# A hybrid encoder layer on one core: program order on all four compute engines through the attention, low halves of w_out and q's norms one step later

## The chip, the cores and the metric

The kernel runs on one core of a Trainium2 chip. Its engines work side by side, each through its own queue in order: PE (TensorE, matrix products; its weight loads are shown as PEld), DVE (VectorE), ACT (ScalarE), POOL (GpSimd), and SP, which only issues transfers. The metric is the device time of one execution in microseconds (us); lower is better.

## The reference

One layer over 16 learned meta tokens and two sequences, 256 and 2048 tokens long, with 1024 channels, in float32. Cut to what matters:

```python
h = rmsnorm(z, norm_w)
q, k, v, g_att, c_val, c_glu, g_conv = split(h @ w_in)      # 512,128,128,512,512,512,512
q, k = rmsnorm(q per head, q_norm_w), rmsnorm(k per head, k_norm_w)
att = windowed_gqa(q, k, v, sink) * silu(g_att)   # 8 heads on 2 kv heads, window 128, ALiBi,
                                                  # every query sees the meta keys and a sink logit
cnv = conformer_conv(c_val, c_glu, ...) * silu(g_conv)      # 31-tap depthwise conv, layernorm, silu
y = z + concat(att, cnv) @ w_out                  # meta tokens dropped
```

## The kernel before, in words

Matrix products of float32 data are made of three passes: each operand is split into a high half (a rounded copy, made on ACT) and a low half (the rest, a subtraction on DVE), and hi x hi, hi x lo and lo x hi are added up in psum.

The tokens are 18 blocks of 128, in groups of three. The **projection** (`c_group`, `g_group`, `kv_group`, `q_group`) goes over units of 256 columns of w_in; the convolution's taps on DVE and the layernorms are threaded in between. q, k, v, gates and the convolution's result go to DRAM (`qd`, `kd`, `vd`, `gd`, `cd`). `attention_open` stands ahead of the last unit, the second half of q for the blocks 9 to 17: nine projections (`proj_te`, 24 matmuls of 256 columns each, tile `pj`). After each of these nine, `spread` runs: after the second it transposes q of block 0 (`q_prep`, tile qT), after the third to ninth it does two slots of the attention each and splits one row block of w_out (`split_wo`, lines 289 to 304: two copies on ACT, two subtractions on DVE, two loads for the next but one).

The **attention** goes in rounds (`slot_step`, 8 slots each). Round r computes the scores of block r (tile S, one of 8 pieces a slot, kv 0 in slots 0 to 3 and kv 1 in 4 to 7), and transposes the probabilities of block r-1 in up to 7 banks (tile pT: three for kv 0, one of the meta keys, three for kv 1; blocks at the ends of a sequence have five). It also does two parts of the output projection a slot (tile y, six matmuls) and, in slot 6, transposes q of the next block. At the end of a slot `tick` counts a clock up by one and runs what earlier steps put off with `later(k, ...)`: k ticks later. The pieces, with their engines:

- S is followed after one tick by `bias_max` on DVE (L382: writes sb, and the row minimum nm), after two by `expo` on ACT (L394; with the kv's last piece also L403), after three (last piece) by `norm` (L406, L407 on DVE, then POOL's L408 and four L417).
- A bank pT is followed after one tick by a high copy on ACT (L451, tile ph) and a low half on DVE (L452, tile pl), after two by the pv matmuls (tile O; the meta bank, with L445, L446 and POOL's L462 `pd`, after three).
- A finished O is merged: a copy on ACT (L505, tile tmp), two additions on DVE (L507), a product on POOL (L513), and two ticks later the split L517 and L518 into `rest`, an operand of the output projection. The convolution's part is multiplied on POOL (L526) and split by L533 and L534.
- A finished y is added to z on DVE (L562) and stored. q's transposes are split by two copies on ACT (L347, L348) and two subtractions on DVE (L349, L350).
- q's norm: ACT squares the projection (L897), DVE sums (L898), POOL takes the root (L122, L123), and `fin` (L916, DVE) multiplies one tick later; the result, one of three buffers, is stored two ticks later by SP.

Psum tags have two buffers each: a for S, b for pT and qT, c for O, d for y; in the last unit the nine `pj` take a, b, d, c, d, c, d, c, d.

**What sets the order.** The tile framework orders the instructions of an engine by a list scheduler that plays the program with estimated durations. `manual_schedule` takes engines out of that: they keep the order in which the program issues. `MAN1` (line 50, POOL) holds from `attention_open` to the start of `attention_rest`, `MAN2` (line 51, POOL and PE) from there to the end. SP is always left to the scheduler, except for single instructions held by `keep_in_program_order`. Ahead of `attention_open` all engines are scheduled.

Of the kernel before, what the change touches and what calls it, by code (L numbers as in the profile page):

```python
# [14 lines left out]
ALU = mybir.AluOpType  # L15
# [31 lines left out]
W0 = 3  # L47
LN_WAIT = (9, 2)
LTAGS = "abdcdcdcd"
MAN1 = {mybir.EngineType.Pool}  # L50
MAN2 = {mybir.EngineType.Pool, mybir.EngineType.PE}
QSLOT = 6
MSLOT = 0
QB = 32
# [15 lines left out]
def blk_local(b):  # L70
    g = b // 3
    return g, (NM if g == 0 else 0) + P * (b % 3)
# [3 lines left out]
def hymba_kernel(  # L76
# [13 lines left out]
    nc = tc.nc  # L90
# [45 lines left out]
    def later(k, f):  # L136
        due.setdefault(clock[0] + k, []).append(f)
# [20 lines left out]
    def store(dst, src):  # L158
        later(2, lambda: nc.sync.dma_start(dst, src))
# [12 lines left out]
    phase = [1]  # L172
# [40 lines left out]
    pool, cst, kw, wo, wo_slot, sbs, wraws = {}, {}, [], {}, {}, [], {}  # L213
# [4 lines left out]
    def attention_open():  # L218
# [4 lines left out]
        cst['man'] = man  # L223
        man.enter_context(tc.manual_schedule(engines=MAN1))
        ap = att_pools.enter_context(tc.tile_pool(name="ap", bufs=2, side="right", reuse_waits="tile"))
# [57 lines left out]
    def load_raw(n):  # L283

        for nh in range(2):
            raw = wraws[n, nh] = pool["a"].tile([P, 512], F32, tag="woraw", name=f"woraw{n}_{nh}", bufs=4)
            tc.keep_in_program_order(nc.sync.dma_start(raw, w_out[OUT_ORDER[n]][:, 512 * nh : 512 * nh + 512]))

    def split_wo(n):

        e = OUT_ORDER[n]
        for hl in range(2):
            idx = 2 * n + hl
            if idx % 3 == 0:
                slot = idx // 3
                wo_slot[slot] = xp.tile([P, ND, 400], F32R, tag=("xh", "xl")[slot % 2], name=f"wo{slot}")
            flat = wo_slot[idx // 3].rearrange("p a n -> p (a n)")
            wo[e, hl] = flat[:, D * (idx % 3) : D * (idx % 3) + D]
        for nh in range(2):
            hi, lo = (wo[e, hl][:, 512 * nh : 512 * nh + 512] for hl in range(2))  # L300
            tc.keep_in_program_order(nc.scalar.copy(hi, wraws[n, nh]))
            tc.keep_in_program_order(nc.vector.tensor_tensor(lo, wraws[n, nh], hi, op=ALU.subtract))  # L302
        if n + 2 < 8:
            later(1, lambda: load_raw(n + 2))

    def load_ga(b):
        gat[b] = pool["b"].tile([P, 4, P], F32, tag="ga", name=f"ga{b}", bufs=1)
# [118 lines left out]
    def plan(b):  # L426
        ks = ([0] if has_left(b) else []) + [1] + ([2] if has_right(b) else [])
        return [(k, 0) for k in ks] + [("m", 0)] + [(k, 1) for k in ks]
# [4 lines left out]
    def bank(b, k, kv):  # L433
        pt = psum.tile([P, 4, P], F32, tag="b", name=f"pT{b}_{k}_{kv}")
        if k == "m":
            for i in range(KV):
                nc.tensor.transpose(pt[:, i, :], pmt[b][:, i].rearrange("p a h m -> p (a h m)"), ident)
        else:
            for hl in range(4):
                nc.tensor.transpose(pt[:, hl, :], sbt[b, kv][:, hl, KCOL[k] : KCOL[k] + P], ident)  # L440

        def split():
            if k == "m":
                ph = pool["a"].tile([P, KV, P], F32R, tag="phm", name=f"phm{b}", bufs=1)
                nc.scalar.copy(ph, pt[:, 0:KV, :])  # L445
                nc.vector.tensor_tensor(ph[64:128], pt[64:128, 0:KV, :], ph[64:128], op=ALU.subtract)  # L446
                later(1, lambda: spread_meta(b, ph))
                return
            ph = pool["a"].tile([P, 4, P], F32R, tag="ph", name=f"ph{b}_{k}_{kv}", bufs=3)
            pl = pool["a"].tile([P, 4, P], F32R, tag="pl", name=f"pl{b}_{k}_{kv}", bufs=3)  # L450
            nc.scalar.copy(ph, pt)  # L451
            nc.vector.tensor_tensor(pl, pt, ph, op=ALU.subtract)  # L452
            pv_st[b, k, kv] = (ph, pl)

        later(1, split)
        later(3 if k == "m" else 2, lambda: pv(b, k, kv))

    def spread_meta(b, ph):

        pd = pool["a"].tile([P, KV, 4, P], F32R, tag="pd", name=f"pd{b}", bufs=1)  # L460
        for kv in range(KV):
            nc.gpsimd.tensor_tensor(  # L462
                pd[:, kv],
                ph[:, kv : kv + 1, :].to_broadcast([P, 4, P]),
                cst["msk"].unsqueeze(2).to_broadcast([P, 4, P]),
                op=ALU.mult,
            )
        pv_st[b, "m"] = pd

    def pv_mm(b, kv, lhs, hs, start, stop):  # L470
        if start:
            opj[b, kv] = psum.tile([P, 4, P], F32, tag="c", name=f"O{b}_{kv}")
        o = opj[b, kv]
        for i, t in enumerate(hs):
            nc.tensor.matmul(o, lhs, t, start=(start and i == 0), stop=(stop and i == 1))  # L475

    def pv_meta(b, kv, stop):
        pin(stop)(nc.tensor.matmul)(
            opj[b, kv], cst["vm"][:, kv, :], pv_st[b, "m"][:, kv], start=False, stop=stop
        )  # L480

    def pv(b, k, kv):
        if k == "m":
            pv_meta(b, 0, True)
            later(1, lambda: merge(b, 0))
            return
        ks = [x for x, y in plan(b) if y == kv and x != "m"]
        first, last = k == ks[0], kv == 1 and k == ks[-1]
        pv_mm(b, kv, vt[b - 1 + k][:, kv, :], pv_st[b, k, kv], first, last)
        if kv == 1 and first:  # L490
            pv_meta(b, 1, False)
        if last:
            later(1, lambda: merge(b, 1))

    def merge(b, kv):
        if "rest" not in cst or (kv == 1 and b not in att):
            return later(1, lambda: merge(b, kv))
        o = opj[b, kv]
        if kv == 0:
            att[b] = pool["b"].tile([P, 4, P], F32, tag="at", name=f"at{b}")  # L500
            mix[b, 1] = (rest_part(2 * (b % 2)), rest_part(2 * (b % 2) + 1))
        at = att[b]
        pr = slice(2 * kv, 2 * kv + 2)
        tmp = pool["b"].tile([64, 4, P], F32, tag="tmp", name=f"tmp{b}_{kv}", bufs=1)
        nc.scalar.copy(tmp, o[64:128])  # L505
        for par in range(2):
            nc.vector.tensor_tensor(  # L507
                at[64 * par : 64 * par + 64, pr, :].rearrange("p a (i q) -> p a i q", q=QB),
                o[0:64].rearrange("p i (a c q) -> p c a i q", a=2, c=2)[:, par],
                tmp.rearrange("p i (a c q) -> p c a i q", a=2, c=2)[:, par],  # L510
                op=ALU.add,
            )
        nc.gpsimd.tensor_tensor(at[:, pr, :], at[:, pr, :], gat[b][:, pr, :], op=ALU.mult)  # L513

        def fin():
            mh, ml = mix[b, 1]
            nc.scalar.copy(mh[:, pr, :], at[:, pr, :])  # L517
            nc.vector.tensor_tensor(ml[:, pr, :], at[:, pr, :], mh[:, pr, :], op=ALU.subtract)  # L518

        later(2, fin)  # L520
# [77 lines left out]
    spread_n = [0]  # L598

    def spread(b):  # L600

        spread_n[0] += 1
        if spread_n[0] == QP:
            q_prep(0)
        upto = EARLY * max(0, spread_n[0] - QP) // (9 - QP)
        while len(slots) > len_all - upto:
            slot_step(*slots.pop(0))
        if 3 <= spread_n[0] <= 8:
            split_wo(spread_n[0] - 3)
        if spread_n[0] == 4:  # L610
            load_mix(0)
        if spread_n[0] == 5:
            load_ga(0)
# [3 lines left out]
    def attention_rest():  # L617
# [4 lines left out]
        cst["man"].close()  # L622
        att_pools.enter_context(tc.manual_schedule(engines=MAN2))
        rest = wl.tile([P, ND, 2, UW], F32R, tag="ws", name="rest")
# [10 lines left out]
    if True:  # L635
# [273 lines left out]
        def q_group(ws, qi, g, after):  # L909
            for b in range(3 * g, 3 * g + 3):  # L910
                ps = proj_te(ws, g, blk_local(b)[1], P)
                rq = head_norm(ps, P, 4, f"q{qi}_{b}")

                def fin(ps=ps, rq=rq, b=b):
                    qs = gp.tile([P, 4, HD], F32, tag="qs", name=f"qs{qi}_{b}")
                    nc.vector.tensor_tensor(  # L916
                        qs,
                        ps[:, :UW].rearrange("p (h e) -> p h e", e=HD),
                        rq.unsqueeze(2).to_broadcast([P, 4, HD]),
                        op=ALU.mult,  # L920
                    )
                    store(qd[b, :, UW * qi : UW * qi + UW], qs.rearrange("p h e -> p (h e)"))

                owe(340)
                later(1, fin)
                tick(24 * 110)
                after(b)

# [132 lines left out]
        for i, (c, u, g) in enumerate(items):  # L1061
# [36 lines left out]
            if c == 0 and u in U_GA:  # L1098
                for k3 in range(3):
                    k = 10 + 3 * (3 * (u - U_GA[0]) + g) + k3  # L1100
# [78 lines left out]
```

## Time and profile before

| what | us |
|---|---|
| median of 3 runs (976.96 to 979.07) | 977.79 |
| the profiled execution's own time | 974.97 |
| its span | 972.8 |
| PE busy | 947.0 |
| DVE busy | 754.1 |
| ACT busy | 422.5 |
| POOL busy | 340.6 |
| load of block 0's q issued at | 582.0 |
| first score reduction of round 1 / 2 / 3 / 4 | 608.8 / 632.6 / 651.9 / 670.2 |
| first score reduction of round 17 | 929.0 |

All times within the execution count from the start of the span. The rows are read so: start, duration, engine, line and operation, output<-inputs, shapes, count, and in brackets how long the engine was idle ahead of it and what ended that. A row with a count merges several instructions that stand together. Windows list the busy time of PE, PEld, DVE, ACT and POOL in a stretch, the granted clock of PE as a share of full speed, the share of time that the DMA engines were busy, and GB/s.

### The profile page before, as it was taken

What the parts mean: (1) busy time and instruction counts of PE and PEld (TensorE: products, weight loads), DVE (VectorE), ACT (ScalarE), POOL (GpSimd) and SP (SyncE); (2) the same over time, 40 slices, a digit from 0 to 9 for tenths busy, and PEclk for the clock granted to TensorE, in tenths of its full rate; (3) what the DMA queues carried; (4) which work ended last, traced back from release to release, by engine and by line L of the source; (5) the groups of instructions that cost most, each with busy time, mean ns of one, the idle gap of its engine ahead of it and who ended that gap; (6) DMA issues with size and microseconds to landing.
All of it is one profiled execution on the core that took longest, in us unless ns stands there. A gap on an engine that the chain in (4) does not pass through costs nothing.

```text
span 972.8 us, 16221 instructions
## 1 busy us (share of the span) xinstructions
PE 947.0 (97%) x5721; PEld 886.3 (91%) x5721; DVE 754.1 (78%) x1261; ACT 422.5 (43%) x1156; POOL 340.6 (35%) x541
## 2 busy tenths in 40 slices
PE   5999999999999999999999998899999999999998
PEld 4999999999999999999999998678888888888886
DVE  4659999998977799999993555867777677767773
ACT  7521121343566710111113455656666666656661
POOL 5600000364467300000002443855445444445442
PEclk9999999999999999999999998999999999999999
DMA  9653354775635221233335639854555445544422
GB/s 332 229 188 117 117 178 172 265 287 189 225 123 174 76 91 74 86 128 136 127 135 179 207 111 258 257 156 126 166 163 164 125 148 170 171 135 127 138 78 76
DMA packets 113872, 155.75 MB, mean 160 GB/s; under 512 B 10592, under 2 KB 77296, under 8 KB 113792
## 3 DMA queue, kind: packets, MB, share of 16 engines
q1 hardware_dynamic: 113648, 154.11, 48.1%
q0 software_dynamic: 144, 0.62, 0.4%
q8 instruction: 45, 0.74, 0.3%
q14 instruction: 35, 0.29, 0.1%
HBM read 101.00 MB, written 54.31 MB: 160 GB/s over the span
## 4 chain that ended last, share of the span: by engine, by line
PE 92%; DMA 2%; DVE 2%; SPq 1%; POOL 1%; issue 1%; ACT 1%; DVEq 0%; POOLq 0%; ACTq 0%
PE pj L780 42%; PE y L551 20%; PE pj L796 14%; PE O L475 5%; PE pT L440 4%; PE S L327 3%; PE O L327 1%; PE lnt L184 1%; DMA wraw<-in_w_in 1%; PE lnu L203 1%; PE qT L327 1%; DMA v<-vd 1%; DMA qd<-qs 1%; DVE wo L302 0%; DVE sb L382 0%
## 5 line engine op out<-in xcount | busy, mean ns | idle before, releaser
L780 PE MATMUL pj<-xh,ws 128*128 128x384 f32 (+1 forms) x1536 | 396.9, 339 | 2.4 <-ACT xh L711 2.4
L863 DVE SCALAR_TENSOR_TENSOR y<-us,cw,y 128x1167 f32<-128x1167 f32 x240 | 328.9, 1425 | 0.6
L780 PEld LDWEIGHTS pj<-xh,ws 128*128 128x128 f32 x1536 | 282.4, 189 | 2.7 <-ACT xh L711 2.7
L780 PE MATMUL pj<-xl,ws 128*128 128x384 f32 (+1 forms) x768 | 262.0, 341 | 0.0
L551 PE MATMUL y<-wo,rest 128*128 128x512 f32 x648 | 173.6, 405 | 0.0
L796 PE MATMUL pj<-ws,xh 128*128 128x256 f32 (+1 forms) x880 | 165.6, 286 | 2.2 <-ACT es L403 1.4
L780 PEld LDWEIGHTS pj<-xl,ws 128*128 128x128 f32 x768 | 144.8, 189 | 0.6 <-DVE xl L720 0.5
L796 PEld LDWEIGHTS pj<-ws,xh 128*128 128x128 f32 (+1 forms) x880 | 137.5, 189 | 3.5 <-ACT sb L394 1.6
L551 PEld LDWEIGHTS y<-wo,rest 128*128 128x128 f32 x648 | 115.2, 189 | 20.4
L796 PE MATMUL pj<-ws,xl 128*128 128x256 f32 (+1 forms) x440 | 125.0, 284 | 0.0
L394 ACT ACTIVATE sb<-sb,nm 128x304 f32<-128x304 f32 (+4 forms) x144 | 77.1, 535 | 63.6 <-DVE nm L382 61.7
L452 DVE TENSOR_TENSOR pl<-pT,ph 128x512 fp32r<-128x512 f32 x100 | 68.5, 685 | 31.8 <-ACT ph L451 31.0
L888 ACT ACTIVATE go<-pj 128x384 f32<-128x384 f32 x48 | 23.6, 491 | 153.9 <-PE pj L780 143.9
L382 DVE CUSTOM_DVE_ANT_0 sb<-S,bias,small 128x304 f32<-128x304 f32 (+4 forms) x144 | 73.1, 511 | 16.0 <-PE S L327 14.9
L796 PEld LDWEIGHTS pj<-ws,xl 128*128 128x128 f32 (+1 forms) x440 | 83.2, 189 | 0.2
L122 POOL TENSOR_SCALAR ssk<-ssk 128x2 f32<-128x2 f32 x18 | 6.4, 354 | 210.9 <-ACT sqk L902 210.8
L417 POOL TENSOR_SCALAR sb<-sb,es 128x304 f32<-128x304 f32 (+4 forms) x144 | 72.1, 519 | 3.5
L451 ACT CAST ph<-pT 128x512 fp32r<-128x512 f32 x100 | 58.0, 581 | 32.8 <-PE pT L440 32.0
L327 PEld LDWEIGHTS S<-kw,q 128*128 128x128 f32 x288 | 53.0, 188 | 13.1 <-DVE nm L382 1.4
L327 PE MATMUL S<-kw,q 128*128 128x304 f32 (+4 forms) x288 | 61.9, 299 | 0.6 <-DVE nm L382 0.6
L440 PE MATMUL pT<-ident,sb 128*128 128x128 f32 x400 | 60.4, 272 | 1.2 <-DVE phm L446 1.1
L122 POOL TENSOR_SCALAR ssq<-ssq 128x4 f32<-128x4 f32 (+2 forms) x55 | 26.4, 480 | 98.1 <-ACT xn L649 76.7
(118 smaller groups left out, 1280.5 us busy)
## 6 DMA issues: line engine op xcount, KB each, us to landing
wd<-ws SPq DMA_DIRECT2D x36, 512.0 KB, 5.7
ws<-wd SPq DMA_DIRECT2D x36, 512.0 KB, 5.3
wraw<-in_w_in SPq DMA_DIRECT2D x52, 256.0 KB, 5.9
xn<-in_z SPq DMA_DIRECT2D x18, 512.0 KB, 5.4
gd<-go SPq DMA_DIRECT2D x48, 192.0 KB, 2.3
yo<-in_z SPq DMA_DIRECT2D x36, 256.0 KB, 4.5
out_y<-yo SPq DMA_DIRECT2D x36, 256.0 KB, 2.7
kw<-kd SPq DMA_DIRECT2D x16, 512.0 KB, 4.6
```

What stands on the lines that cost most here:

```text
L327: r = f(*a, **k)
L382: nc.vector.tensor_tensor_reduce(out=sb[:, n, c0:c1], in0=ps[:, 0:w], in1=cst["bias"][:, kv, n, c0 - QB * n : c1 - QB * n], scale=1.0, sca ...
L394: nc.scalar.activation(sb[:, n, c0:c1], sb[:, n, c0:c1], AF.Exp, bias=nm[:, n : n + 1], scale=-1.0, accum_out=rs[:, n : n + 1],)
L417: nc.gpsimd.tensor_scalar(sb[:, k, a0:a1], sb[:, k, a0:a1], es[:, k : k + 1], 1.0, op0=ALU.mult, op1=ALU.mult)
L440: nc.tensor.transpose(pt[:, hl, :], sbt[b, kv][:, hl, KCOL[k] : KCOL[k] + P], ident)
L451: nc.scalar.copy(ph, pt)
L452: nc.vector.tensor_tensor(pl, pt, ph, op=ALU.subtract)
L475: nc.tensor.matmul(o, lhs, t, start=(start and i == 0), stop=(stop and i == 1))
L551: nc.tensor.matmul(ps, mh[mi][:, e % 4, :], wo[e, wi][:, cols], start=(e == 4 and k == 0), stop=(e == 3 and k == 2),)
L780: nc.tensor.matmul(ps[:, :n], ws[:, d, wi, P * half_i : P * half_i + P], x[xi][:, d, o : o + n], start=(k == 0), stop=(k == 3 * ND - 1),)
L796: nc.tensor.matmul(ps[:rows, :UW], x[xi][:, d, o : o + rows], ws[:, d, wi, :], start=(k == 0), stop=(k == 3 * ND - 1),)
L863: nc.vector.scalar_tensor_tensor(y[:, yo + o0 : yo + o1], u[:, o0 + k : o1 + k], cw[:, j, k : k + 1], y[:, yo + o0 : yo + o1], op0=ALU.mul ...
```

## The change

Five edits, and none adds or removes an instruction:

1. `MAN1` and `MAN2` become the set of all four compute engines: from `attention_open` to the end, PE, ACT and DVE keep the program's order as POOL did.
2. In `split_wo` the two low halves of w_out are put off, the first by one tick and the second by two; the loads for the next but one follow the second low half.
3. The pv matmuls of block 0 come three ticks after their bank and not two.
4. In `spread`, `split_wo` stands ahead of the slots' work and not behind it.
5. q's norm `fin` comes `phase[0]` ticks later: one before `attention_open`, as it was, and two in the last unit.

```diff
-MAN1 = {mybir.EngineType.Pool}
-MAN2 = {mybir.EngineType.Pool, mybir.EngineType.PE}
+MAN1 = {getattr(mybir.EngineType, e) for e in ("Pool", "PE", "Activation", "DVE")}
+MAN2 = MAN1
...
             tc.keep_in_program_order(nc.scalar.copy(hi, wraws[n, nh]))
-            tc.keep_in_program_order(nc.vector.tensor_tensor(lo, wraws[n, nh], hi, op=ALU.subtract))
-        if n + 2 < 8:
-            later(1, lambda: load_raw(n + 2))
+
+            def low(nh=nh, hi=hi, lo=lo):
+                tc.keep_in_program_order(nc.vector.tensor_tensor(lo, wraws[n, nh], hi, op=ALU.subtract))
+                if nh == 1 and n + 2 < 8:
+                    load_raw(n + 2)
+
+            later(1 + nh, low)
...
-        later(3 if k == "m" else 2, lambda: pv(b, k, kv))
+        later(3 if k == "m" or b == 0 else 2, lambda: pv(b, k, kv))
...
         upto = EARLY * max(0, spread_n[0] - QP) // (9 - QP)
+        if 3 <= spread_n[0] <= 8:
+            split_wo(spread_n[0] - 3)
         while len(slots) > len_all - upto:
             slot_step(*slots.pop(0))
-        if 3 <= spread_n[0] <= 8:
-            split_wo(spread_n[0] - 3)
...
-                later(1, fin)
+                later(phase[0], fin)
```

How the order moves is shown at three places. The lines of the changed kernel are four higher from line 308 on (L394 is L398 there, L451 is L455). First ACT, from slot 3 of a round on to slot 0 of the next, before; ph_0_1 is the copy of key block 0 for kv 1, rs the row sum that the exponential writes:

```order
L403 ACTIVATE es_0_8288<-nm_0_8286,small 128x4
L451 CAST ph_0_1_8411<-pT_0_1_8389 128x512
L451 CAST ph_1_1_8445<-pT_1_1_8417 128x512
L394 ACTIVATE sb_5962,rs_1_8401<-sb_5962,nm_1_8400 128x304
L505 COPY tmp_0_8480<-O_0_8331 64x512
L394 ACTIVATE sb_5962,rs_1_8401<-sb_5962,nm_1_8400 128x304
L451 CAST ph_2_1_8486<-pT_2_1_8455 128x512
```

The same stretch in the changed kernel:

```order
L407 ACTIVATE es_0_8288<-nm_0_8286,small 128x4
L455 CAST ph_0_1_8411<-pT_0_1_8389 128x512
L398 ACTIVATE sb_5962,rs_1_8401<-sb_5962,nm_1_8400 128x304
L455 CAST ph_1_1_8445<-pT_1_1_8417 128x512
L398 ACTIVATE sb_5962,rs_1_8401<-sb_5962,nm_1_8400 128x304
L509 COPY tmp_0_8480<-O_0_8331 64x512
L455 CAST ph_2_1_8486<-pT_2_1_8455 128x512
```

Each exponential has moved one place up, ahead of the copy of the next bank (or of tmp_0). Next ACT again, from q's split in slot 6 over the end of the round, before:

```order
L348 CAST q_10_8475<-qT_8470 64x4x4x32
L394 ACTIVATE sb_5962,rs_1_8401<-sb_5962,nm_1_8400 128x304
L533 CAST rest<-cn_8387 128x512
L505 COPY tmp_1_8538<-O_1_8439 64x512
L451 CAST ph_0_0_8543<-pT_0_0_8514 128x512
L394 ACTIVATE sb_5962,rs_1_8401<-sb_5962,nm_1_8400 128x304
L403 ACTIVATE es_1_8402<-nm_1_8400,small 128x4
L451 CAST ph_1_0_8577<-pT_1_0_8550 128x512
L517 CAST rest<-at_8479 128x256
L394 ACTIVATE sb_5969,rs_0_8527<-sb_5969,nm_0_8526 128x304 x2
```

And in the changed kernel:

```order
L352 CAST q_10_8475<-qT_8470 64x4x4x32
L398 ACTIVATE sb_5962,rs_1_8401<-sb_5962,nm_1_8400 128x304
L521 CAST rest<-at_8479 128x256
L398 ACTIVATE sb_5962,rs_1_8401<-sb_5962,nm_1_8400 128x304
L407 ACTIVATE es_1_8402<-nm_1_8400,small 128x4
L509 COPY tmp_1_8538<-O_1_8439 64x512
L455 CAST ph_0_0_8543<-pT_0_0_8514 128x512
L398 ACTIVATE sb_5969,rs_0_8527<-sb_5969,nm_0_8526 128x304
L537 CAST rest<-cn_8387 128x512
L455 CAST ph_1_0_8577<-pT_1_0_8550 128x512
```

The round's last exponential with its L403 has moved ahead of tmp_1 and ph_0_0, the next round's first ahead of the convolution's copy and ph_1_0. Last, SP in the opening, behind the eight loads of `vm`, before (qs_9 is the normed q of block 9, on its way to `qd`; q_6111 is the load of block 1's q):

```order
L257 DMA vm<-vmd 16x256 x8
L159 DMA qd<-qs_9_6030 128x256
L281 DMA q_6111<-qd 128x512
L269 DMA kw_5948<-kd 128x4x128
L271 DMA kw_5948<-kd 128x4x128
L277 DMA v_6115<-vd 128x256
L159 DMA qd<-qs_10_6064 128x256
```

And in the changed kernel:

```order
L257 DMA vm<-vmd 16x256 x8
L281 DMA q_6111<-qd 128x512
L269 DMA kw_5948<-kd 128x4x128
L271 DMA kw_5948<-kd 128x4x128
L277 DMA v_6115<-vd 128x256
L159 DMA qd<-qs_9_6062 128x256
L159 DMA qd<-qs_10_6102 128x256
```

The store of block 9's q has gone behind the four loads of block 1. On PE, in the same stretch, the four transposes of block 0's q have moved from the start of the fifth of the nine last projections to the place between the second and the third, and S_0_0 and S_0_1 from within the sixth to right behind the third; each later pair of scores follows the next projection.

## The prediction

> **What bounds the kernel now.** I read first the busy shares of the page, then the table of windows over the attention, then DVE's order of time for the period of a round, then the rows of ACT and DVE inside one round.
>
> ```profile
> PE 947.0 (97%) x5721; PEld 886.3 (91%) x5721; DVE 754.1 (78%) x1261; ACT 422.5 (43%) x1156; POOL 340.6 (35%) x541
> 600.00:625.00 25.00, 19.05 (x98) 15.42 (x97) 20.54 (x56) 17.82 (x50) 14.36 (x21) 0.80 0.90 296
> 625.00:650.00 25.00, 22.85 (x123) 18.95 (x122) 18.65 (x49) 15.29 (x41) 15.07 (x24) 1.00 0.54 159
> 700.00:750.00 50.00, 50.00 (x272) 42.45 (x272) 38.20 (x96) 32.56 (x84) 23.03 (x35) 1.00 0.54 167
> 670.24 0.53 DVE L382 CUSTOM_DVE_ANT_0 sb<-S,bias,small 128x304 f32<-128x304 f32 x1
> 928.98 0.49 DVE L382 CUSTOM_DVE_ANT_0 sb<-S,bias,small 128x272 f32<-128x272 f32 x1
> ```
>
> The columns of a window are PE, PEld, DVE, ACT and POOL busy time, then the clock granted. In the attention's rounds PE is never idle (50.00 of 50) at full clock, and a round costs what PE needs. The two L382 rows are the first score reduction of rounds 4 and 17; between them lie 13 rounds: (928.98 - 670.24) / 13 = 19.90 us each. The change adds no arithmetic, so it can make a round longer only by making PE wait. In the opening (600 to 650) PE loses 5.95 + 2.15 = 8.1 us, and the clock falls to 0.80 on average; a better order could win there.
>
> **Term 1, the rounds.** PE and POOL were in program order here already; new is program order on ACT and DVE. The order of ACT (shown with the change) is the point. In each slot a tick issues the exponential of the slot before (L394), then this slot's copy (L451), then on DVE the low half (L452) and this slot's reduction (L382). In program order these are queued so on both engines, and each waits for the one ahead: L382 of slot t-1, L394, L451, L452, L382 of slot t. That is a closed loop through two in-order engines, and PE is not in it. Before, four copies were queued ahead of exponentials that they do not need (ph_1_1, tmp_0, tmp_1 with ph_0_0, ph_1_0), which cuts the loop. I add it up with starts from one round of before, whose durations repeat in every round:
>
> ```profile
> 741.09 0.59 ACT L505 COPY tmp<-O 64x512 f32<-64x512 f32 x1 [0.58 <-PE O L327]
> 741.70 0.85 DVE L507 TENSOR_TENSOR at<-O,tmp 64x256 f32<-64x256 f32 x2
> 745.55 0.68 DVE L349 TENSOR_TENSOR q<-qT,q 64x512 fp32r<-64x512 f32 x1 [0.65 <-ACT q L348]
> 746.10 0.60 ACT L533 CAST rest<-cn 128x512 fp32r<-128x512 f32 x1
> 746.25 0.69 DVE L350 TENSOR_TENSOR q<-qT,q 64x512 fp32r<-64x512 f32 x1
> 746.98 0.53 DVE L382 CUSTOM_DVE_ANT_0 sb<-S,bias,small 128x304 f32<-128x304 f32 x1
> 748.04 0.84 DVE L507 TENSOR_TENSOR at<-O,tmp 64x256 f32<-64x256 f32 x2
> 748.91 0.69 DVE L452 TENSOR_TENSOR pl<-pT,ph 128x512 fp32r<-128x512 f32 x1
> ...
> 754.33 0.55 ACT L394 ACTIVATE sb<-sb,nm 128x304 f32<-128x304 f32 x1 [1.46 <-DVE nm L382]
> 754.87 0.35 ACT L445 CAST phm<-pT_m 128x256 fp32r<-128x256 f32 x1
> 755.26 0.43 DVE L446 TENSOR_TENSOR phm<-pT_m,phm 64x256 fp32r<-64x256 f32 x1 [0.97 <-ACT phm L445]
> 756.10 0.53 DVE L382 CUSTOM_DVE_ANT_0 sb<-S,bias,small 128x304 f32<-128x304 f32 x1 [0.41 <-PE S L327]
> 756.68 0.55 ACT L394 ACTIVATE sb<-sb,nm 128x304 f32<-128x304 f32 x1 [1.45 <-DVE nm L382]
> 757.23 0.28 ACT L403 ACTIVATE es<-nm,small 128x4 f32<-128x4 f32 x1
> 757.42 0.56 ACT L451 CAST ph<-pT 128x512 fp32r<-128x512 f32 x1
> 758.01 0.69 DVE L452 TENSOR_TENSOR pl<-pT,ph 128x512 fp32r<-128x512 f32 x1
> 758.62 0.68 DVE L562 TENSOR_TENSOR yo<-y,yo 128x512 f32<-128x512 f32 x1
> 759.22 0.52 DVE L382 CUSTOM_DVE_ANT_0 sb<-S,bias,small 128x304 f32<-128x304 f32 x1
> ```
>
> From start to start: L382 to L394 0.58 (756.10, 756.68); L394 to a copy 0.54 (754.33, 754.87), with L403 between 0.74; L451 to L452 0.59; L452 to the next on DVE 0.61; L562 to L382 0.60; L505 to L507 0.61; both L507 to L452 0.87. The stretch 756.10 to 759.22 is slot 3 to slot 4; its order is the same before and after, and it already shows this loop at work, 3.12 us of it. The eight steps of a round after the change, each from one L382 to the next:
>
> - slot 0 to 1: 0.58 + 0.54, L533 0.60, 0.59 + 0.61 = 2.92
> - 1 to 2: 0.58 + 0.54 + 0.59 + 0.61 = 2.32
> - 2 to 3, the meta bank: 0.58 + 0.54 + 0.39 + 0.43 = 1.94
> - 3 to 4: 3.12, read off
> - 4 to 5, with the second L562: 2.32 + 0.60 = 2.92
> - 5 to 6, tmp_0 and both L507 between: 0.58 + 0.54 + 0.61 + 0.87 + 0.61 = 3.21
> - 6 to 7, no bank but q's split: L382 to L349 0.53, 0.70, 0.73 = 1.96
> - 7 to 0, L403, tmp_1, both L507: 0.58 + 0.74 + 0.61 + 0.87 + 0.61 = 3.41
>
> The sum is 21.80 us against PE's 19.90. PE cannot run ahead of it for long: the transposes' psum tag has two buffers, so a bank waits for the L452 of two slots back, and a pv matmul waits for its own L452. So a round becomes 21.8 us, PE idles 1.9 us of it in pieces under about 1 us, and 13 rounds cost 13 x 1.90 = 24.7 us. Of rounds 2, 3 and 17 (five banks, or narrower scores) I count 1.3 us more: **+26 us**. Eight steps known to some 0.08 us each way give 1.3 to 2.5 us a round, 17 to 33 us; if the loop is slacker than I see, the bound is 0.
>
> What else moves in a round is covered: L518 and L534 come one or two rows later, the mix is read several slots later; es_0 becomes ready some 2 us later, and POOL's scaling is needed only in the next round.
>
> **Term 2, the opening.** Here PE, too, leaves the scheduler's order, in which q's transposes stood after the fourth of the last nine projections and the scores later still. In program order qT of block 0 follows the second (its square is the ACT row at 582.18), and the scores of block 0 the third.
>
> ```profile
> 582.18 0.39 ACT L897 ACTIVATE sqq<-pj 128x256 f32<-128x256 f32 x1 [0.56 <-PE pj L796]
> 582.02 0.42 SPq L281 DMA_DIRECT2D q<-qd  x1
> q<-qd SPq DMA_DIRECT2D x5, 256.0 KB, 2.9
> 589.19 0.58 ACT L348 CAST q<-qT 64x512 fp32r<-64x512 f32 x1
> 590.29 0.69 DVE L349 TENSOR_TENSOR q<-qT,q 64x512 fp32r<-64x512 f32 x1
> 590.99 0.69 DVE L350 TENSOR_TENSOR q<-qT,q 64x512 fp32r<-64x512 f32 x1
> 595.79 0.37 SPq L159 DMA_DIRECT2D qd<-qs  x1
> 597.62 0.42 DVE L916 TENSOR_TENSOR qs<-pj,rqq 128x256 f32<-128x256 f32 x1 [2.42 <-DMA qd<-qs]
> 597.92 0.62 SPq L277 DMA_DIRECT2D v<-vd  x1
> 603.19 0.55 PE L796 MATMUL pj<-ws,xh 128*128 128x256 f32 x1 [1.35 <-ACT es L403]
> 602.00:604.00 2.00, 0.81 (x4) 0.84 (x5) 1.38 (x5) 1.97 (x9) 0.00 (x0) 0.50 0.91 291
> ```
>
> - qT waits for its load: issued at 582.02, landing after 2.9 us, while PE is free from about 582.1: 2.8 us idle. Before, two more projections lay in between.
> - The scores wait for q's split, which program order puts behind the third projection's square: 0.39 + two copies of 0.58 (L347 and L348) + 0.69 + 0.69 = 2.9, with hand-overs about 3.1 us in which PE has nothing else to run.
> - The store of block 9's q goes behind four loads on SP, from 595.79 to about 598.2; DVE's L916 of block 12 needs that buffer and waited for it already (2.42 us, to 597.62). With the same 1.8 us it lands at 600.0. Behind it on DVE stand two low halves of w_out (0.68 each, like L452) and two score reductions, which free the psum buffers of S_1_0 and S_1_1; PE is through with the fifth projection at about 598.2: some 4 us idle.
>
> By about 603 us PE has then done five of the last nine projections and six of block 0's eight scores; before, it stood at the eighth's start (the PE row at 603.19). That is behind by two projections of 24 matmuls, 2.8 us each, and about 1 us of scores: 6.7 us. From there both orders have gates (8.1 us of idle in the two windows, half clock at 602 to 608); I add 1.3 us for w_out's low halves, now ahead of block 1's reductions. **+8 us**; bounds 0, where the new gaps only replace the old ones, and +16, where the later gates lengthen as the first do.
>
> The rest of the edits (the low halves and reload a tick later, block 0's pv a step later, the split ahead of the slot's work, q's norm one tick later) is inside this sum: same counts, same durations, no instruction more.
>
> **Sum.** The profiled execution took 974.97 us (span 972.8). 974.97 + 26 + 8 = 1009; the median of the runs, 977.79, lies 2.8 above it, so I forecast **1012 us** for the median.
>
> **The rivals.**
> - *Only the opening is lost.* The loop is cut by slack that I do not see, for instance a copy that starts sooner after L394, and the rounds stay on PE. For it: before, the steps 1 to 3 met PE's pace. Against it: 3 to 4 is the loop itself, at 3.12. 977.8 + 8 = 986 us. Chance 0.08.
> - *Faster.* One mechanism: program order closes the gaps of the opening, the 8.1 us of idle and some 3 us that half clock takes from 602 to 608 (half of 6). It decides only if the round's loop stays at or under PE's 19.90, that is if my eight steps are 9% too long, and q's load lands before PE gets to it. 977.8 - 11 = 967 us. Chance 0.06.
> - *Nothing to measure*, within 0.2% (about what a measurement of this kernel can tell from no change, 2 us): the two terms cancel. Chance 0.03. That the order is not changed at all is out: the rows of ACT show it.
> - *The clock falls in the rounds.* The row at 602 shows 0.50 after two gaps of about 1.3 us with little work between, so PE's clock can drop. Price: if half of each round ran at half clock, PE would need 19.9 x 1.5 = 29.9 us, 10 us a round, near 1140 us. Against it: after the gap that follows the meta bank the clock stayed up:
>
> ```profile
> 635.64 0.33 PE L437 MATMUL pT_m<-ident,pm 128*128 128x128 f32 x1 [2.09 <-POOL pm L408]
> 635.00:640.00 5.00, 4.36 (x24) 3.71 (x25) 1.63 (x5) 1.98 (x6) 4.14 (x7) 1.00 0.14 52
> ```
>
>   2.09 us idle and still 1.00, and the new gaps are shorter, with PE busy 91%. Chance 0.03. The Trainium skill, "TensorE: Matmul & The Clock Gate", speaks for this rival in its section on a second failure mode (frequent short idles while psum buffers cycle make the clock swing between half and full) and against it in the one on oscillation (an idle stretch of about 3.4 us is needed); by the first the sum would be that of this rival, by the second nothing changes. The rows at 635 agree with the second, those at 602 with neither alone.
>
> **How the numbers follow.** The forecast, both terms, has 0.80; its own range is 977.8 + 17 + 0 = 995 to 977.8 + 33 + 16 = 1027. The range reaches to the first rival and a little above: 986 to 1030. Slower by over 0.2%: 0.80 + 0.08 + 0.03 = 0.91; within: 0.03; faster: 0.06.
>
> **What would show it.** Right: L382 of slot 0 returns every 21.8 us in rounds 4 to 16, each ACT exponential waits for DVE's nm, and PE waits for L452 in every round, at clock 1.00. Opening: PE idle before the first qT, the first S, and block 0's S_1_0. Wrong: rounds at 19.9 with no PE waits (term 1 falls), or the first S of round 2 at 633 us or sooner (term 2).

## The result, and the profile after

The changed kernel takes **1021.3 us** (median of 4 runs, 1019.89 to 1023.38), beside 978.4 us for the kernel before in the same comparison (976.96 to 979.1): ratio 1.0451, 95% interval 1.0426 to 1.0476. It is slower by 43 us. The forecast was 1012 us, 986 to 1030. The profiled execution after took 1019.89 us, its span 1018.1; before, they were 974.97 and 972.8. Lines of the changed kernel are four higher from line 308 on, so L382, L394, L451, L452 are L386, L398, L455, L456, and L327, L475, L897, L916 are L331, L479, L901, L920. L302, in `split_wo`, is L304; L301 keeps its number.

First three lines of the page after: the busy shares, the head of the chain of work that ended last, and the group of exponentials (busy time, mean ns of one | idle time ahead of it, and what ended it).

```profile
PE 963.8 (95%) x5721; PEld 888.2 (87%) x5721; DVE 755.3 (74%) x1261; ACT 417.2 (41%) x1156; POOL 345.6 (34%) x541
...
PE 64%; DVE 17%; ACT 8%; issue 5%; DMA 3%; SPq 1%; POOL 1%; POOLq 0%; DVEq 0%; ACTq 0%
...
L398 ACT ACTIVATE sb<-sb,nm 128x304 f32<-128x304 f32 (+4 forms) x144 | 76.9, 534 | 173.9 <-DVE nm L386 173.8
```

The same group before:

```profile
L394 ACT ACTIVATE sb<-sb,nm 128x304 f32<-128x304 f32 (+4 forms) x144 | 77.1, 535 | 63.6 <-DVE nm L382 61.7
```

The 144 exponentials last as long as before (76.9 and 77.1 us), but ACT now stands idle 173.9 us ahead of them, always for DVE's row minimum nm. A quarter of the chain is DVE and ACT (17% + 8%), with reductions, low halves, copies and exponentials in it. PE shows only 17 us more busy time (963.8 against 947.0) in a span 45 us longer.

Next, three windows of the rounds after (PE, PEld, DVE, ACT, POOL busy with their counts, granted clock, DMA share, GB/s):

```profile
700.00:750.00 50.00, 47.25 (x245) 38.09 (x244) 33.66 (x87) 28.40 (x75) 21.93 (x33) 1.00 0.50 153
750.00:800.00 50.00, 47.11 (x243) 37.79 (x241) 33.42 (x88) 27.46 (x74) 23.12 (x36) 1.00 0.44 135
800.00:850.00 50.00, 47.73 (x250) 38.92 (x249) 32.33 (x86) 27.42 (x74) 22.31 (x33) 1.00 0.42 127
```

PE's waits after from 686 to 960 us, where this row is the only one (what waited for what: us in total, times, longest):

```profile
PE O L479 <- DVE pl L456: 13.9, 38, 0.5
```

The first rows of the same view from 575 to 650 us:

```profile
PE S L331 <- ACT wo L301: 4.1, 1, 4.1
PE qT L331 <- DMA q<-qd: 2.8, 1, 2.8
PE O L479 <- DVE pl L456: 2.7, 3, 1.6
PE S L331 <- ACT sqq L901: 2.5, 1, 2.5
```

In the rounds PE is idle in every window, and what it waits for there is the low half of p (L456), at a clock of 1.00 throughout. In the opening it waits for q's load and, ahead of score matmuls, for work of ACT.

Where the 45.3 us of the span went is read from the first score reduction of rounds 2, 4 and 17 (DVE in order of time, after):

```profile
643.51 0.38 DVE L386 CUSTOM_DVE_ANT_0 sb<-S,bias,small 128x176 f32<-128x176 f32 x1
...
686.12 0.52 DVE L386 CUSTOM_DVE_ANT_0 sb<-S,bias,small 128x304 f32<-128x304 f32 x1
...
973.05 0.49 DVE L386 CUSTOM_DVE_ANT_0 sb<-S,bias,small 128x272 f32<-128x272 f32 x1
```

| stretch | before, us | after, us | more, us |
|---|---|---|---|
| start of the span to round 2 (opening) | 632.60 | 643.51 | 10.9 |
| rounds 2 and 3 | 37.64 | 42.61 | 5.0 |
| rounds 4 to 16 (13 rounds) | 258.74 | 286.93 | 28.2 |
| first reduction of round 17 to the end | 43.82 | 45.05 | 1.2 |

A round of the middle stretch went from 258.74 / 13 = 19.90 us to 286.93 / 13 = 22.07 us.

### The profile page after: what moved, and what is told of

It reads as the page before. It is cut to its first block, busy times and chain, and to the rows that moved or that the text cites. A ratio compares the mean times of both kernels' runs of the same rounds, so it can differ in the third digit from the quotient of the medians.

```text
span 1018.1 us, 16213 instructions
## 1 busy us (share of the span) xinstructions
PE 963.8 (95%) x5721; PEld 888.2 (87%) x5721; DVE 755.3 (74%) x1261; ACT 417.2 (41%) x1156; POOL 345.6 (34%) x541
## 4 chain that ended last, share of the span: by engine, by line
PE 64%; DVE 17%; ACT 8%; issue 5%; DMA 3%; SPq 1%; POOL 1%; POOLq 0%; DVEq 0%; ACTq 0%
PE pj L784 38%; PE pj L800 12%; PE y L555 7%; DVE sb L386 4%; DVE pl L456 4%; DVE at L511 2%; ACT sb L398 2%; PE O L479 2%; ACT tmp L509 2%; DVE yo L566 1%; PE pT L444 1%; ACT ph L455 1%; DVE q L354 1%; DVE q L353 1%; PE S L331 1%
## 5 line engine op out<-in xcount | busy, mean ns | idle before, releaser
L398 ACT ACTIVATE sb<-sb,nm 128x304 f32<-128x304 f32 (+4 forms) x144 | 76.9, 534 | 173.9 <-DVE nm L386 173.8
L456 DVE TENSOR_TENSOR pl<-pT,ph 128x512 fp32r<-128x512 f32 x100 | 68.9, 689 | 52.7 <-ACT ph L455 51.9
L421 POOL TENSOR_SCALAR sb<-sb,es 128x304 f32<-128x304 f32 (+4 forms) x144 | 79.2, 567 | 3.6
L331 PEld LDWEIGHTS S<-kw,q 128*128 128x128 f32 x288 | 53.3, 191 | 24.0 <-ACT wo L301 4.3
L386 DVE CUSTOM_DVE_ANT_0 sb<-S,bias,small 128x304 f32<-128x304 f32 (+4 forms) x144 | 73.0, 508 | 1.6 <-PE S L331 0.5
L331 PE MATMUL S<-kw,q 128*128 128x304 f32 (+4 forms) x288 | 63.2, 302 | 10.3 <-ACT wo L301 4.1
L479 PE MATMUL O<-pl,v 128*128 128x512 f32 x100 | 44.6, 446 | 18.6 <-DVE pl L456 18.6
```

The source lines that it names most:

```text
L331: r = f(*a, **k)
L386: nc.vector.tensor_tensor_reduce(out=sb[:, n, c0:c1], in0=ps[:, 0:w], in1=cst["bias"][:, kv, n, c0 - QB * n : c1 - QB * n], scale=1.0, sca ...
L398: nc.scalar.activation(sb[:, n, c0:c1], sb[:, n, c0:c1], AF.Exp, bias=nm[:, n : n + 1], scale=-1.0, accum_out=rs[:, n : n + 1],)
L421: nc.gpsimd.tensor_scalar(sb[:, k, a0:a1], sb[:, k, a0:a1], es[:, k : k + 1], 1.0, op0=ALU.mult, op1=ALU.mult)
```

## The experiments

Theory at the outset: two causes, each with its place. In the rounds, program order on ACT and DVE closes a loop (reduction, exponential, the next bank's copy, its low half, the next reduction) that is longer than PE's round. In the opening, PE's own place in line makes q's transposes and the scores wait. Rivals: the loss is of the opening alone and the rounds only run late behind it; the edits other than the order cost it; one of the two engines' orders costs by itself; in the opening it is ACT's and DVE's order, and not PE's.

All were compared with the kernel before on the same chip. "Round 2" is the start of its first score reduction, "round" the mean of the 13 rounds from 4 to 16, both read as in the table above.

| kernel | median, us | ratio and 95% interval | round 2 at, us | round, us |
|---|---|---|---|---|
| before (profile) | 977.8 | 1 | 632.6 | 19.90 |
| after | 1021.3 | 1.0451 (1.0426 to 1.0476) | 643.5 | 22.07 |
| opening in order, edits, rounds as before | 983.5 | 1.0062 (1.0042 to 1.0081) | 642.6 | 19.90 |
| rounds in order alone | 1012.4 | 1.0357 (1.0341 to 1.0372) | 635.9 | 22.07 |
| after, exponential last in its step | 986.6 | 1.0092 (1.0076 to 1.0107) | 643.5 | 19.88 |
| after without the four edits | 1021.0 | 1.0445 (1.0429 to 1.0460) | 645.2 | 22.07 |
| ACT alone in order in the rounds | 976.5 | 0.9996 (0.9983 to 1.0009) | 636.2 | 20.00 |
| DVE alone in order in the rounds | 975.5 | 0.9992 (0.9979 to 1.0006) | 634.2 | 19.88 |
| the four edits alone | 977.2 | 1.0002 (0.9989 to 1.0014) | 634.4 | 19.90 |
| opening in order, no edits | 985.1 | 1.0090 (1.0073 to 1.0107) | 644.6 | 19.90 |
| PE alone in order in the opening | 977.3 | 1.0001 (0.9990 to 1.0012) | 633.7 | 19.90 |
| ACT and DVE alone in order in the opening | 985.9 | 1.0088 (1.0074 to 1.0103) | 643.8 | 19.90 |
| opening in order, edits, q later | 988.9 | 1.0120 (1.0104 to 1.0135) | 649.1 | 19.90 |
| opening in order, edits, norm later | 982.5 | 1.0064 (1.0047 to 1.0081) | 640.9 | 19.90 |

### Which stretch costs what

The opening in order, the rounds as before:

```diff
 (the kernel after)
-MAN2 = MAN1
+MAN2 = {mybir.EngineType.Pool, mybir.EngineType.PE}
```

> The kernel after, with ScalarE and VectorE left to the scheduler again in the rounds (MAN2 is GpSimd and TensorE, as before); the opening stays in program order with its four edits. Theory (the two in-order engines close a loop over the steps of a round): a round goes back from 22.07 to about 19.9 us, 13 rounds give back 28, rounds 2 and 3 and the tail most of their 6; what is left is the opening's 10.9, so about 989 us (987 to 994, 1.011 of the kernel before). Rival (the order of the opening is the cost and the rounds only run late behind it): over 1010 us.

It gave 983.5 us with rounds of 19.90: the rounds' loss is gone. That is less than the 987 to 994 forecast, though the first reduction of round 2 stands at 642.6, only 1 us ahead of the kernel after. The forecast took the opening's 10.9 us from two profiles, and the profiled execution before, 974.97 us, was a quick one beside medians of 976.0 to 978.4. The three kernels below with no edit and the opening's engines as before start round 2 at 634.2 to 636.2; beside these, the kernel after is 7.3 to 9.3 us late there.

The rounds in order, the opening as before:

```diff
 (the kernel before)
-MAN2 = {mybir.EngineType.Pool, mybir.EngineType.PE}
+MAN2 = {getattr(mybir.EngineType, e) for e in ("Pool", "PE", "Activation", "DVE")}
```

> The kernel before, with ScalarE and VectorE put in program order in the rounds alone (MAN2 is all four engines, MAN1 GpSimd as before, none of the other edits). Theory: a round takes 22.07 us, 13 rounds add 28 and the edges up to 6, so about 1009 us (1005 to 1014, 1.031), with the first score's maximum of round 2 still near 632.6. Rival (the edits to w_out and q or the opening set the rounds back): rounds of 19.9 us and about 980 us.

It gave 1012.4 us and rounds of 22.07. The two parts add up: 3.57% here and 0.90% for the opening in order without the edits make 4.47%, beside 4.51% for the kernel after and 4.45% for the one with both orders and no edits.

That last one asks what the four edits do:

```diff
 (the kernel before)
-MAN1 = {mybir.EngineType.Pool}
-MAN2 = {mybir.EngineType.Pool, mybir.EngineType.PE}
+MAN1 = {getattr(mybir.EngineType, e) for e in ("Pool", "PE", "Activation", "DVE")}
+MAN2 = MAN1
```

> The kernel before with only the two sets of ordered engines changed to all four: program order from the opening to the end without the four edits (low halves of w_out, block 0's values one step later, split of w_out ahead of the slot, q's norms one step later). Theory: rounds of 22.07 us as after; the edits lie in the opening alone, where they take TensorE's waits for q's norms and for w_out's halves off the queue, so 1021 to 1035 us. Rival (the edits themselves set the opening back): under 1018 us.

1021.0 us, the kernel after's 1021.3 within the intervals: at the lower end of the forecast, and here no sign that the edits take anything off. The edits alone, under the old sets of engines:

```diff
 (the kernel after)
-MAN1 = {getattr(mybir.EngineType, e) for e in ("Pool", "PE", "Activation", "DVE")}
-MAN2 = MAN1
+MAN1 = {mybir.EngineType.Pool}
+MAN2 = {mybir.EngineType.Pool, mybir.EngineType.PE}
```

> The four edits alone (low halves of w_out and reload later, block 0's values one step later, the split of w_out ahead of the slots, q's norms one step later), with the two sets of ordered engines as before. Theory: the scheduler orders the opening's work anyhow, so they change little: 974 to 983 us. Rival (the edits make the opening late, not its order): 983 to 990 us with the first reduction of round 2 over 638.

977.2 us, ratio 1.0002. So the four edits cost nothing, and the order is the whole change.

### What closes the loop in the rounds

If the loop is what the prediction says, it opens when the exponential no longer stands ahead of the copy on ACT, with all four engines still in program order. A second list of steps put off, run at the end of a tick, does that (the exponential then stands behind ph and q's copies of its tick):

```diff
 (the kernel after)
+    def at_end(k, f):
+        due_end.setdefault(clock[0] + k, []).append(f)
...
         for f in due.pop(clock[0], []):
             f()
+        for f in due_end.pop(clock[0], []):
+            f()
...
-        later(2, expo)
+        at_end(2, expo)
```

> The kernel after, all four engines in program order, but the exponential of a slot is issued at the end of its step instead of ahead of the high half of p and the copies of q: on ScalarE it then stands behind the work that VectorE waits for in this step, so that the loop spans two steps. Theory (it is the place of the exponential in ScalarE's queue that closes the loop): rounds near 19.9 us, about 990 us (986 to 996). Rival (any fixed order on ScalarE and VectorE costs it, since the steps differ in work): rounds stay over 21 us and the time over 1005 us.

986.6 us, rounds of 19.88. ACT's and DVE's rows of one slot there, in order of time (L460 is the copy, L403 the exponential, L461 the low half, L391 the reduction):

```profile
701.34 0.59 ACT L460 CAST ph<-pT 128x512 fp32r<-128x512 f32 x1
701.82 0.56 ACT L403 ACTIVATE sb<-sb,nm 128x304 f32<-128x304 f32 x1
702.41 0.68 DVE L461 TENSOR_TENSOR pl<-pT,ph 128x512 fp32r<-128x512 f32 x1
703.02 0.53 DVE L391 CUSTOM_DVE_ANT_0 sb<-S,bias,small 128x304 f32<-128x304 f32 x1
```

Its group of exponentials, and one window of its rounds:

```profile
L403 ACT ACTIVATE sb<-sb,nm 128x304 f32<-128x304 f32 (+4 forms) x144 | 77.0, 535 | 14.5 <-DVE nm L391 13.9
```

```profile
700.00:750.00 50.00, 50.00 (x272) 42.45 (x271) 36.43 (x95) 30.18 (x83) 25.73 (x38) 1.00 0.50 147
```

The copy starts ahead of the exponential, so the low half waits for no reduction of the slot before. ACT's idle time ahead of exponentials falls from 173.9 to 14.5 us, and PE is busy 50.00 of 50 again. Moving the exponential alone gives back 35 of the 43 us; the rival, that any fixed order costs it, falls. The edit moves the exponentials of the opening too, and there it wins nothing: round 2 starts at 643.5, as in the kernel after (at a lower granted clock from 575 to 650 us, 0.84 beside 0.91, so a small gain could be hidden).

The loop runs through two engines, so each alone should be able to cut it. ACT alone in order:

```diff
 (the kernel before)
-MAN2 = {mybir.EngineType.Pool, mybir.EngineType.PE}
+MAN2 = {getattr(mybir.EngineType, e) for e in ("Pool", "PE", "Activation")}
```

> The kernel before with ScalarE alone added to the ordered engines of the rounds; VectorE stays with the scheduler, which then queues it nearly in program order, but with the low half of slot 0 behind slot 0's reduction. Theory (the exponential ahead of the copy in ScalarE's queue closes the loop, and VectorE's order is close to program order in any case): the loop loses only its step into slot 0, so rounds of 20.5 to 21.5 us and 986 to 1004 us. Rival (VectorE's order is what costs): rounds of 19.9 us and 978 to 981 us.

A miss: 976.5 us and rounds of 20.00. By this number alone the rival, that DVE's order is what costs, would stand. The opposite run, DVE alone:

```diff
 (the kernel before)
-MAN2 = {mybir.EngineType.Pool, mybir.EngineType.PE}
+MAN2 = {getattr(mybir.EngineType, e) for e in ("Pool", "PE", "DVE")}
```

> The kernel before with VectorE alone added to the ordered engines of the rounds; ScalarE stays with the scheduler, which queues four copies ahead of the exponentials of the slots before them. Theory: the loop is cut on ScalarE, rounds of 19.9 to 20.1 us and 978 to 984 us. Rival (VectorE's order is what costs): rounds over 21 us and over 995 us.

975.5 us and rounds of 19.88: neither order costs by itself. What the expectation for ACT alone got wrong is what the scheduler does with DVE. In slot 5 of a round there (L451 the copy, L452 the low half):

```profile
743.91 0.57 ACT L451 CAST ph<-pT 128x512 fp32r<-128x512 f32 x1
744.00 0.69 DVE L562 TENSOR_TENSOR yo<-y,yo 128x512 f32<-128x512 f32 x1 [0.67 <-PE y L551]
744.61 0.52 DVE L382 CUSTOM_DVE_ANT_0 sb<-S,bias,small 128x304 f32<-128x304 f32 x1
745.05 0.08 DVE L382 DVE_READ_ACCUMULATOR2_ANT nm<- 128x1 f32 x1
745.05 0.68 DVE L452 TENSOR_TENSOR pl<-pT,ph 128x512 fp32r<-128x512 f32 x1
```

The copy is through at 744.48, yet DVE runs the reduction first and the low half after it. In slot 0, where the expectation had it, it does the same. So the next exponential does not stand behind this low half, and the loop is cut on DVE. Both orders are needed to close it, which is what a loop through two queues means, and what neither single run shows by itself.

### The opening

Without the edits, all four engines in order in the opening and the rounds as before:

```diff
 (the kernel before)
-MAN1 = {mybir.EngineType.Pool}
+MAN1 = {getattr(mybir.EngineType, e) for e in ("Pool", "PE", "Activation", "DVE")}
```

> The kernel before with all four engines in program order in the opening alone, without the four edits; the rounds as before. Theory: TensorE's place in the opening's order is the cost, as in the run with free rounds (983.5 us); without the edits the first reduction of round 2 comes near 645 and the time is 983 to 990 us, with rounds of 19.9. Rival (the edits are the cost in the opening): 976 to 981 us.

985.1 us, with round 2 at 644.6, as the theory had it. With the edits it was 983.5 (1.0062 beside 1.0090, the intervals just overlapping), so whether the edits win something in an ordered opening stays open. And so far nothing tells PE's order from that of ACT and DVE. Two runs do, PE alone and the other two alone:

```diff
 (the kernel before)
-MAN1 = {mybir.EngineType.Pool}
+MAN1 = {mybir.EngineType.Pool, mybir.EngineType.PE}
```

> The kernel before with TensorE alone added to the ordered engines of the opening; ScalarE and VectorE stay with the scheduler there, the rounds as before. Theory (TensorE's place in line makes q's transposes wait for the load and the scores for q's split and for w_out's halves): most of the opening's loss is here, 981 to 987 us, the first reduction of round 2 at 640 us or later. Rival (ScalarE's and VectorE's order makes the opening late): 975 to 979 us.

```diff
 (the kernel before)
-MAN1 = {mybir.EngineType.Pool}
+MAN1 = {getattr(mybir.EngineType, e) for e in ("Pool", "Activation", "DVE")}
```

> The kernel before with ScalarE and VectorE in program order in the opening and TensorE left to the scheduler there, the rounds as before. Theory: TensorE runs projections in its gaps again, 975 to 980 us, the first reduction of round 2 under 638 us. Rival (ScalarE's and VectorE's order makes the opening late): 982 to 987 us.

PE alone: 977.3 us, ratio 1.0001. ACT and DVE alone: 985.9 us, 1.0088, the whole loss of the opening in order. The theory falls for the opening. PE's waits from 575 to 650 us with PE alone in order:

```profile
PE S L327 <- ACT wo L301: 3.2, 1, 3.2
PE qT L327 <- DMA q<-qd: 2.7, 1, 2.7
PE O L475 <- DVE pl L452: 1.5, 2, 0.9
PE S L327 <- DVE nm L382: 1.0, 1, 1.0
PE O L327 <- DVE es L406: 0.7, 1, 0.7
PE pT_m L437 <- POOL pm L408: 0.6, 1, 0.6
```

and with ACT and DVE alone in order:

```profile
PE pj L796 <- DVE es L406: 3.7, 1, 3.7
PE O L475 <- ACT ph L451: 3.7, 2, 2.1
PE S L327 <- ACT sb L394: 2.5, 1, 2.5
PE O L475 <- DVE pl L452: 2.4, 1, 2.4
PE qT L327 <- DMA q<-qd: 2.2, 1, 2.2
PE pT_m L437 <- POOL pm L408: 1.6, 1, 1.6
PE pT L440 <- DVE phm L446: 1.5, 1, 1.5
PE O L327 <- POOL pd L462: 0.3, 1, 0.3
PE y L551 <- DVE mcl L534: 0.3, 1, 0.3
```

The first list has the two waits on which the prediction built, 2.7 us for q's load and 3.2 us ahead of the scores, and its sum is 9.7 us. The kernel before waited about as long in the same stretch, 9.5 us over nine rows, the longest 2.1 us for POOL's pm: the waits that PE takes early it no longer has later. The second list sums to 18.2 us, and all but q's load and the two of POOL are for ACT and DVE. So it is the products of these two that come late.

The granted clock is a rival here, since it falls in the opening of every kernel. Over 575 to 650 us it was 0.93 before, 0.91 with PE alone and 0.91 after; with the opening in order it was 0.93 with the edits, 0.86 without them, and 0.89 with ACT and DVE alone. The run with the edits still loses 0.62% at the clock of the kernel before, so the clock is not the cause there; in the other two it can carry a part.

Two runs looked for one wait behind this, both from the kernel with the opening in order, the edits, and the rounds as before. The first moves block 0's q behind two more projections, as the scheduler had done:

```diff
-QP = 2
+QP = 4
```

> The kernel with free rounds (opening in program order with the four edits, rounds as before; 983.5 us) with one number changed: block 0's q is transposed after the fourth of the last nine projections instead of after the second, and the first slots follow it. Theory (q's load and q's split are what TensorE waits for): the 2.8 us ahead of the transposes goes, and with it some of the wait ahead of the scores, 976 to 981 us. Rival (the scores, two projections later, only move the wait to block 1's): 983 us or more.

988.9 us, 5 us slower, with round 2 at 649.1. The wait for q's load is gone from PE's list, and that wins nothing. Why the run is slower is not shown: ahead of scores PE waits 6.6 us for the row minimum (3.6 in the kernel it started from) and 8.8 us for nothing that the profile shows (4.0), and the granted clock from 575 to 650 us was 0.82 beside 0.93. The second moves the norm of q:

```diff
-                later(phase[0], fin)
+                later(3 if phase[0] == 2 else 1, fin)
```

> The kernel with free rounds (opening in program order with the four edits, rounds as before; 983.5 us) with q's normalization in the opening one more step later, so that on VectorE it stands behind a slot's low half of w_out and score reduction instead of in front of them; everything stays in program order in the opening. Theory (VectorE, in order, waits some 1.4 us a block for GpSimd's 1/rms ahead of each q, 5.8 us over seven blocks, and the score reductions stand behind it): these waits fall under 2 us in all, the first reduction of round 2 comes by 639, and the time is 976 to 980 us. Rival (the wait only moves: to the sums of squares, w_out's loads or the projections' psum banks, held a step longer): 982 us or more.

DVE's first waits from 584 to 645 us but for one load, in the kernel that this started from:

```profile
DVE qs L920 <- POOL rqq L123: 5.8, 7, 1.4
DVE ssq L902 <- ACT sqq L901: 5.1, 2, 2.6
DVE qs L920 <- DMA qd<-qs: 3.9, 1, 3.9
```

and with the norm later:

```profile
DVE ssq L902 <- ACT sqq L901: 6.4, 4, 2.3
DVE qs L920 <- DMA qd<-qs: 3.4, 1, 3.4
```

The seven waits for POOL's rqq are gone, 5.8 us of them, and the time is 982.5 us, ratio 1.0064 beside 1.0062. Round 2 starts 1.7 us earlier, and nothing of that is seen in the ratio. The rival holds: DVE now waits longer for ACT's sqq (6.4 us) and for w_out's copies (2.4 us, 0.6 in the kernel it started from). Which of the waits of ACT and DVE in the opening sets its end is left open: shown is only that their order costs it (0.88%), and that PE's order alone does not; taking away the wait for q's load or the one for rqq won nothing. DVE's wait for the store of q's buffer, the 3.9 us above, is not needed for the loss either: from 575 to 645 us it is 4.0 us in the kernel before, and the two ordered openings without edits (1.0090 and 1.0088) show none of it. One difference was not tried: from 585 to 645 us ACT idles 16.0 us ahead of exponentials for DVE's row minimum in the kernel after and 18.0 with ACT and DVE alone in order, against 5.9 before and 6.1 with PE alone.

No kernel beats the one before by more than its interval. The two with one engine more in order in the rounds are level with it.

## Why the prediction was right, point by point

- **The sign and the place: right.** A loop through ACT's and DVE's queues, with PE outside it, sets the rounds. It is shown three ways: closed alone it costs 3.57%, cut on ACT by one moved line the rounds are back at 19.88 us, and with either engine free they are at 19.88 to 20.00.
- **The eight steps: right in kind, 0.27 us short in sum.** They measured 3.05, 2.31, 1.96, 3.12, 2.92, 3.33, 1.99 and 3.39 us, 22.07 in all, where the prediction had 2.92, 2.32, 1.94, 3.12, 2.92, 3.21, 1.96 and 3.41, together 21.80. Two steps make up the difference. The first, slot 0 to 1, and the start of the second, in the kernel after (DVE's and ACT's rows in order of time):

```profile
774.41 0.53 DVE L386 CUSTOM_DVE_ANT_0 sb<-S,bias,small 128x304 f32<-128x304 f32 x1
...
774.98 0.55 ACT L398 ACTIVATE sb<-sb,nm 128x304 f32<-128x304 f32 x1 [1.48 <-DVE nm L386]
...
775.53 0.60 ACT L537 CAST rest<-cn 128x512 fp32r<-128x512 f32 x1
776.04 0.58 ACT L455 CAST ph<-pT 128x512 fp32r<-128x512 f32 x1
776.16 0.77 DVE L538 TENSOR_TENSOR rest<-cn,rest 128x512 fp32r<-128x512 f32 x1 [0.93 <-ACT rest L537]
...
776.86 0.68 DVE L456 TENSOR_TENSOR pl<-pT,ph 128x512 fp32r<-128x512 f32 x1
777.46 0.52 DVE L386 CUSTOM_DVE_ANT_0 sb<-S,bias,small 128x304 f32<-128x304 f32 x1
...
788.33 0.55 ACT L398 ACTIVATE sb<-sb,nm 128x304 f32<-128x304 f32 x1 [1.80 <-DVE nm L386]
789.00 0.58 ACT L509 COPY tmp<-O 64x512 f32<-64x512 f32 x1
```

  The copy is through at 776.62, but the low half starts at 776.86, behind L538, which stands ahead of it on DVE. The prediction called that instruction (L534 before) covered and counted only its partner on ACT. In the step from slot 5 to 6, the last two rows, the copy of O starts 0.67 us after the exponential (788.33 to 789.00) and not 0.54. Over 13 rounds the steps make 28.2 us where the prediction had 24.7.
- **The edges, mis-sized.** "Of rounds 2, 3 and 17 (five banks, or narrower scores) I count 1.3 us more" was 6.2 (5.0 and 1.2). PE needs less there, 37.64 / 2 = 18.8 us a round before, while the loop took 42.61 / 2 = 21.3: it shrinks less than PE's work (by 0.8 us against 1.1), so these rounds lost more than the others, and not less. The 5.0 may be 4.3 to 7.0, since the kernels with rounds of 19.9 to 20.0 us take 35.6 to 38.3 us for rounds 2 and 3.
- **Term 2, right in size (8 us predicted, 10.9 in the profile), wrong in mechanism.** The step that failed is "Here PE, too, leaves the scheduler's order", with its idle times for q's load (2.8 us, measured 2.8) and ahead of the scores (3.1, measured 4.1). These waits came, and with PE alone in order they cost nothing (1.0001). The loss is ACT's and DVE's order (1.0088); that the size came out near is luck. Of the third wait, some 4 us ahead of S_1_0, PE shows 1.12 us ahead of it and 0.56 ahead of S_1_1. By medians the opening costs less than the 10.9 us of the profile: 983.5 less 978.0 is 5.5 us with the edits, 985.1 less 976.9 is 8.2 without.
- **The edits, counted as "inside this sum": right.** Alone they are 1.0002.
- **The sum, 9 us short.** The two terms make 34 us where the medians differ by 43. The rounds were 3.5 us short and the edges 4.9, so 1021 us is inside the range, well above the forecast of 1012.
- **The rivals.** The clock stayed at 1.00 in every window from 700 to 850 us, so it did not fall in the rounds. The Trainium skill, "TensorE: Matmul & The Clock Gate", section "A second HAM failure mode: psum-queue depth-cycling", has frequent short idles swing the clock between half and full in another kernel; it does not say how frequent they must be. No such swing shows here, with 38 waits of at most 0.5 us from 686 to 960 us and a clock of 1.00 in every window. "Only the opening is lost" would have been right had the loop been cut: the run with free rounds (983.5 us) and the one with the exponential last (986.6) are that case, near the rival's 986.

## What to carry to other kernels

Program order on two engines that hand work back and forth can close a loop that no single engine's busy share shows: add up one turn of it, start to start, with every instruction that stands in either queue, and compare it with the bound engine's period. Issue the work that the other engine waits for ahead of the work that waits for the other engine, and the loop spans two steps. A wait that one engine takes early is no loss by itself; take the order of one engine at a time and see which costs.

## What was not expected of the hardware

PE's idle time in the profile understates what it lost. In the three windows from 700 to 850 us its idle time after is 2.75 + 2.89 + 2.27 = 7.9 of 150 us, or 5.3%, while the count of its rows fell from 272 + 272 + 273 = 817 to 245 + 243 + 250 = 738, or 9.7%, which fits the rounds (19.90 / 22.07 is 9.8% less). Two rows after show how that comes about:

```profile
784.73 0.39 PE L479 MATMUL O<-ph,v 128*128 128x512 f32 x1
784.96 0.40 PE L479 MATMUL O<-pl,v 128*128 128x512 f32 x1
```

Two matmuls in flight start 0.23 us apart, and each is shown 0.39 to 0.40 us long. Where the next one is late, the first 0.17 us of the delay lie under the end of the one before and count as busy. Compare counts of instructions in a window, or periods, rather than busy shares. The Trainium skill says the same of one matmul in "TensorE: Matmul & The Clock Gate", section "Single matmul latency": a constant tail of some 175 ns beyond the streaming time. The 0.17 us here lies near it, but the profile models the ends of matmuls, so this is no measurement of the tail; what the counts show is the work that was not done.

In the opening the granted clock is down without a long stop: over 600 to 625 us it was 0.80 in the kernel before, where PE's longest wait shown from 575 to 625 us is 1.4 us (for L403). It fell to 0.64 from 601 to 602 us and 0.50 after that, when PE had been busy for 3.3 of the 6 us from 597 to 603, in pieces.
